# q, k, v and both mLSTM streams split into high and low parts before they go to DRAM

## The chip, the cores and the metric

The kernel runs on one core of a Trainium2 chip. The metric is the device time of one execution in microseconds (us), the median over runs.

## What is computed

One layer of a hybrid encoder for one sequence of 1024 tokens with 1024 channels, in float32: two feed-forward blocks around two sequence mixers. The mixers are a differential attention with 8 heads (two score maps of 64 channels in each, rotary q and k, a block-causal mask over chunks of 64) and an mLSTM with 4 heads of 256 channels.

```
h = x + 1/2 * g1 * SwiGLU_1(mod(rms(x)))
u = mod(rms(h));  P = u @ W_in
...
def mlstm_branch(xm, o_pre, conv_w, conv_b, w_mq, w_mk, w_mv, w_if, b_if, ml_skip, g_mlnorm):
    xc = jax.nn.silu(causal_conv(xm, conv_w, conv_b))
    q = jnp.einsum('bshd,hde->bhse', xch, w_mq)
    k = jnp.einsum('bshd,hde->bhse', xch, w_mk)
    v = jnp.einsum('bshd,hde->bhse', xmh, w_mv)
    ...
    y = (hn + ml_skip.reshape(H, Dh) * xch) * jax.nn.sigmoid(o_pre).reshape(B, S, H, Dh)
...
def diff_attention(q, k, v, lam, g_subln, lambda_init):
    q = rope(q)
    k = rope(k)
    ...
        s = jnp.einsum('bqhcd,bkhcd->bchqk', qi, k) * scale
        p = jax.nn.softmax(s, axis=-1)
        a = p[:, 0] - lam * p[:, 1]
        return jnp.einsum('bhqk,bkhd->bqhd', a.astype(v.dtype), v)
```

## The kernel before

**High and low parts.** A float32 product is done on TensorE as three products of two operands that are each written as a high part (the value rounded to the type fp32r) and a low part (what is left). The three are lines 132, 133 and 134 (`mm3`): high by high, low by high, high by low. A split costs one cast on ScalarE and one subtraction on VectorE. `split` (lines 137 and 138) reads its source from another tile; `split_in` (lines 143 and 144) works on a tile that a load has just filled, and leaves the low part in its place.

**Order.** TensorE's order is the order in which the program is written. ScalarE, VectorE, GpSimd and SyncE's DMA issues are ordered by the tile framework's scheduler. Nearly all DMAs are issued by SyncE (SP), in one order, and one that waits holds up those behind it. A tile that a DMA reads or writes comes free only when that DMA has landed.

**Stages** (times of the profiled execution). The first feed-forward block runs to 693 us. Then `stage_in`: projections to the mLSTM's input xm, channel tile by channel tile. `conv` copies the product from PSUM into `xp`, runs four VectorE passes of a causal convolution into `acc`, a SiLU (line 743) gives xc, and both are split into the four tiles `xh` for the gate products `gates` (lines 754 and 756). The tiles `xh` have one buffer each. xc and xm are stored to DRAM in float32 (lines 746 and 747). The output-gate projections run to 894 us, with the last four `gates` at the half and at the end of the first two of them. The gate chain, a row of small steps and DMAs on the gate values, runs beside these.

From 895 us the mLSTM (`stage_mlstm`) and from 1206 to 1745 us the attention (`stage_attn`) run with dense work (projections to q, k, v and branch gates, in `job_*`) put between their steps: `paced` writes items in the order of due times and dense pieces between them. `mlstm_head` loads 256 tokens of xm or xc at a time, one DMA (line 1051) and one `split_in` for each. `vps` (lines 1084 to 1086) are the products of xm to the mLSTM's values; each is split into `mv`. `job_v` stores the attention's v in float32 (lines 906 and 908), `rotate` the rotated q and k of half the tokens of a head (lines 930 to 945; its inputs `qa` and its three tiles `t`).

In the attention, each head's q goes twice into `Q` (rows 0 to 63 become the high part, 64 to 127 the low part) and k twice into `Kl`, split into `Kh` and `Kl`. The first 256 columns are loaded (line 1245) when the head before has done its last scores with them, the other 768 behind that. Scores `sc` are lines 1276 and 1277; ScalarE's exponential (line 1281) gives `p`; `pt` (line 1305) are transposes of p, which are split into `ah` and `al` (lines 137 and 138) and multiplied with v (`av`) into `po`.

The tiles `t` of 128x512 float32, whoever takes them (`self.t512()`), come from one ring of six buffers.

Of the kernel before, what the change touches and what calls it, by code (L numbers as in the profile page):

```python
# [39 lines left out]
class Halves:  # L40
    """two tiles with half of the tokens each"""
# [9 lines left out]
class Net:  # L51
# [40 lines left out]
    # conditioning: one column block of w_ada per call  # L92
# [27 lines left out]
    # weights  # L120
# [19 lines left out]
    def split_in(self, hi, lo):  # L140
        """the same of what has been loaded into the place of the low part"""
        raw = lo.bitcast(F32)
        self.nc.scalar.copy(hi, raw)
        self.nc.vector.tensor_sub(lo, raw, hi.bitcast(F32))

    def set_lnexp(self, after):
        """have the table set with Ln and Exp loaded behind `after`"""
        t = self.nc.scalar.preload_act_table_set(LNEXP)
        self.after(t, after)
        return t  # L150
# [6 lines left out]
    def rstd_of(self, ps, n, last):  # L157
        """1 / sqrt(ps / n + eps); `last`: the activation before it"""
# [9 lines left out]
    # 1 / rms over channels, on every partition, for some of the tokens  # L168
# [35 lines left out]
    def sum_square(self, n, i, m):  # L204
        """add channel tile m of half n, its i-th, to the running sum of squares"""
        nc = self.nc
        sq = self.t512()
        self.sq_last = nc.scalar.activation(sq, self.h[m][:, n * NW:n * NW + NW], AF.Square)
        if i:
            nc.vector.tensor_add(sq, self.sq_acc, sq)  # L210
        self.sq_acc = sq
# [12 lines left out]
    def norm_step(self, i, q, j, bank):  # L224
        """first half's modulation behind the steps of the last products"""
# [8 lines left out]
    def norm_behind(self, i, n, m, bank):  # L234
        """behind the update of channel tile m of half n: statistics, and the first half's modulation"""
# [12 lines left out]
    def group(self, srcs, psp, tag, hook):  # L248
        """several M-tiles of a projection of u at once, channel tile by channel tile"""
# [15 lines left out]
    def ffn(self, wgu, wd, gt, first, plain, hid, after, step, extra=None):  # L265
        """h += gate * (silu(u w_gate) * (u w_up)) w_down; hidden passes through DRAM"""
# [33 lines left out]
    # The hidden layer goes to DRAM as the operands that down() takes: even tiles are its rows b1., odd ones b2.  # L300
# [9 lines left out]
    def store_right(self, hid, f, c2):  # L310
        """what follows from the second token half of tile f"""
# [8 lines left out]
    def store_left(self, hid, f, c1):  # L320
        """what follows from the first token half, behind store_right"""
# [10 lines left out]
    # One level of Strassen's scheme in Winograd's form: 7 products for the 8 of two tiles of w^T u, with  # L332
    # w^T = [a11 a12; a21 a22] (tiles x channel halves) and u = [b11 b12; b21 b22] (channel x token halves)
# [10 lines left out]
    def combine_u(self, x, pool):  # L344
        """t1 = b12 - b11, t2 = b22 - t1, -t4 = b21 - t2 for one channel tile of each half"""
# [20 lines left out]
    def combine_u3(self, x):  # L366
        """t3 = b22 - b12, in the place of b12"""
# [69 lines left out]
    def down(self, wd, gt, hid, psg, tp, after, step):  # L437
        """the same scheme for w_down^T (channel halves x even and odd tiles) and the hidden layer"""
# [63 lines left out]
        # product: its operands, weights to fetch meanwhile, a combination that takes a weight's place  # L502
# [43 lines left out]
    def first_start(self, srcs, psg, gtag, psd, dtag):  # L546
        """the first block's input: statistics, modulation and the first tiles as x and w_ada come in"""
# [42 lines left out]
    def first_norm(self, i, srcs, psg, gtag, psd, dtag):  # L590
        """later blocks' input: the first tiles run on one half while the other is normalised"""
# [8 lines left out]
    def out_tail(self, n, i, m, bank):  # L600
        """final norm behind the last update of h"""
# [36 lines left out]
    # one M-tile of a projection of u: PSUM halves  # L638
# [18 lines left out]
    def mix_setup(self):  # L657
# [4 lines left out]
                                 for j in range(FT // 2)] for i in range(2))  # L662
# [3 lines left out]
        self.xcd, self.xmd, self.od, self.ybd = ([sc(f"{c}{h}", [P, 2, T]) for h in range(4)]  # L666
                                                 for c in ("xc", "xm", "so", "yb"))
        self.qkd = [sc(f"qk{h}", [2, 2, 2, 32, T]) for h in range(8)]
        self.vd = [sc(f"v{h}", [P, 2, 8, P]) for h in range(4)]
# [4 lines left out]
    def fold_gates(self, hd, psp, tag):  # L674
        """gate weights seen from xc and xm, as [hi | lo] stationary tiles"""
# [32 lines left out]
    def stage_in(self, st):  # L708
        """xm with causal conv and gate pre-activations; sigmoid of the output gate"""
# [15 lines left out]
    def conv_o(self, s1, psd, psg, pre):  # L725
# [3 lines left out]
        def conv(j, ps):  # L729
# [17 lines left out]
            nc.sync.dma_start(out=self.xmd[j // 2][:, j % 2], in_=xp[:, 4:4 + T])  # L747
# [140 lines left out]
    # dense work that fills the tensor engine between the steps of the two sequence mixers  # L888
    def job_v(self, hp):
        nc = self.nc  # L890
        w = [self.unit(self.a["wv"][hp, i]) for i in range(2)]
        for tt in range(8):
# [3 lines left out]
            for k in range(KT):  # L896
# [5 lines left out]
                if k % 2:  # L902
                    if k == KT - 1:
                        if tt % 2 == 0:
                            vo = self.rope.tile([P, 2, 2, P], F32, name=self.nm("vo"), tag=f"vo{tt // 2 % 2}")
                        nc.scalar.copy(vo[:, :, tt % 2], o.rearrange("p (q c) -> p q c", q=2))
                        if tt % 2:
                            nc.sync.dma_start(out=self.vd[hp][:, :, tt - 1:tt + 1], in_=vo)
                    yield 6 * 0.11

    def job_qk(self, hd):
        """rotary q and k of a head"""
# [20 lines left out]
    def rotate(self, hd, ns, a, ps):  # L933
# [10 lines left out]
        for h, t in enumerate((x, a)):  # L944
            nc.sync.dma_start(out=self.qkd[hd][:, :, h].rearrange("q c r t -> (q c) r t")[:, :, ns], in_=t)

    def job_g(self, s, j):
        """pre-activation of a branch gate; for the second one -log of its sigmoid"""
# [29 lines left out]
    def job_b(self, n, m):  # L978
        """gated mLSTM branch of the merge"""
# [19 lines left out]
    def chunk(self):  # L999
        """a piece of the dense work; its time on the tensor engine, 0 when none is left"""  # L1000
# [12 lines left out]
    def paced(self, items):  # L1013
        """emit items (due, time, function) by due time, dense work in between"""
# [29 lines left out]
    def mlstm_head(self, hd, before, pitch, items, m1, m2, psS, psR, psN):  # L1044
# [4 lines left out]
        def load(dst, src, cs):  # L1049
            hi, lo = (x[:, :, cs] for x in dst)  # L1050
            nc.sync.dma_start(out=lo.bitcast(F32), in_=src[:, :, cs])
            self.split_in(hi, lo)

        def load_xc(c):
            load(self.xc, self.xcd[hd], slice(c * 256, c * 256 + 256))

        def begin():
            for c in (3, 2, 1, 0):
                load(self.xm, self.xmd[hd], slice(c * 256, c * 256 + 256))
# [5 lines left out]
        def begin_qk():  # L1065
            """scores of a head: q k^T = xc (w_q w_k^T) xc^T"""
# [114 lines left out]
        # blocks of queries and of keys go from the last to the first, so that the next head's keys and  # L1181
        # values can take the place of those that have had their last use
# [46 lines left out]
    def stage_attn(self, dense):  # L1229
        nc, tc = self.nc, self.tc  # L1230
        nlam, gcol = self.lam[:, 2:3], self.lam[:, 3:4]
        with tc.tile_pool(name="a1", bufs=1) as a1, tc.tile_pool(name="a2", bufs=2) as a2, \
# [7 lines left out]
            def load(hd, part):  # L1240
                """some columns of q (twice, for its high and low parts) and of k (twice)"""
                for x, dst in ((0, qs), (1, kl)):
                    src = self.qkd[hd][x].rearrange("c x r t -> (x r) c t")[:, :, part]
                    for r in (0, 64):
                        nc.sync.dma_start(out=dst[r:r + 64, :, part].bitcast(F32), in_=src)
                self.split_in(kh[:, :, part], kl[:, :, part])
                for o in range(part.start, part.stop, 256):
                    cs = slice(o, o + 256)
                    t = self.t512().rearrange("p (c t) -> p c t", c=2)[64:128]
                    self.split_in(t.bitcast(F32R), qs[64:128, :, cs])  # L1250
                nc.scalar.copy(qs[0:64, :, part], qs[0:64, :, part].bitcast(F32))

            def load_v(hd):
                v = [a2.tile([P, 8, P], F32R, name=self.nm("av"), tag=f"av{i}", bufs=1) for i in range(2)]
                nc.sync.dma_start(out=v[1].bitcast(F32), in_=self.vd[hd // 2][:, hd % 2])
                self.split_in(v[0], v[1])
# [325 lines left out]
```

## Time and profile before

| | |
|---|---|
| time, median of 3 runs | 2677.02 us (2673.28 to 2679.34) |
| span of the profiled execution | 2681.1 us |
| busy: TensorE / VectorE / ScalarE | 97% / 70% / 48% of the span |
| chain that ended last | TensorE 84%, DMA 7%, VectorE 5%, ScalarE 3% |
| granted TensorE clock, mean | 0.990 |

TensorE is busy nearly all the time, so what the kernel can lose or win lies in the places where TensorE stands. The profiled execution is 4.1 us (0.15%) longer than the median of the runs; the page shows no time of it besides its span.

### The profile page before, as it was taken

The page shows a single profiled execution, that of the slowest core. Times are in us where ns is not written, and L with a number is a line of the kernel's source. Part 1 is how long each engine was busy: PE and PEld are TensorE (multiplying, and loading weights), DVE is VectorE, ACT ScalarE, POOL GpSimd, SP SyncE. Part 2 cuts the span into 40 slices and gives each one's busy share as a digit, 9 for nine tenths or more (in the row PEclk, how much of TensorE's full clock was granted, in tenths as well). Part 3 has the DMA queues.
Part 4 walks back from the last instruction along what each step waited for, and adds up shares of the span by engine and source line. Part 5 has one row for each costly group of instructions (what it writes and reads, how often), then busy time and mean ns, then how long its engine had stood idle before and what let it go on. Part 6 is the DMA issues. An engine that isn't in the chain of part 4 may idle for free.

```text
span 2681.1 us, 35203 instructions
## 1 busy us (share of the span) xinstructions
PE 2592.6 (97%) x12704; PEld 2155.8 (80%) x12704; DVE 1877.3 (70%) x3352; ACT 1288.3 (48%) x2369; POOL 22.5 (1%) x85
## 2 busy tenths in 40 slices
PE   6999999999899999999999999999999999999998
PEld 4888887778777799997777778777887888888886
DVE  7987878678795456646766766654467776766867
ACT  6333333446435366654666766753345332323444
POOL 0000000000000000000000000000000000000000
PEclk8999999999999999999999999999999999999999
DMA  7434345833674423334333333558342333236533
GB/s 262 162 130 145 118 149 185 274 99 104 215 258 149 140 91 118 111 100 121 111 102 106 99 105 115 159 198 277 131 140 87 110 98 115 99 102 216 161 95 122
DMA packets 174471, 380.47 MB, mean 142 GB/s; under 512 B 18405, under 2 KB 47529, under 8 KB 174297
## 3 DMA queue, kind: packets, MB, share of 16 engines
q1 hardware_dynamic: 174296, 378.24, 43.6%
q8 instruction: 99, 1.62, 0.2%
q14 instruction: 76, 0.61, 0.1%
HBM read 280.27 MB, written 97.90 MB: 141 GB/s over the span
## 4 chain that ended last, share of the span: by engine, by line
PE 84%; DMA 7%; DVE 5%; ACT 3%; issue 1%; SPq 0%; DVEq 0%; ACTq 0%; POOL 0%; POOLq 0%
PE gu L134 10%; PE gu L133 10%; PE gu L132 10%; PE acc L132 5%; PE acc L133 5%; PE acc L134 5%; PE ab L132 2%; PE ab L133 2%; PE ab L134 2%; PE dn L134 2%; PE dn L132 2%; PE dn L133 2%; PE gp L132 2%; PE gp L134 2%; PE gp L133 2%; PE pt L1305 1%
## 5 line engine op out<-in xcount | busy, mean ns | idle before, releaser
L132 PE MATMUL gu<-uh,wh 128*128 128x512 f32 x800 | 314.2, 393 | 10.1 <-ACT uh L201 8.8
L133 PE MATMUL gu<-ul,wh 128*128 128x512 f32 x800 | 313.4, 392 | 1.3 <-DVE ul L202 1.3
L134 PE MATMUL gu<-uh,wl 128*128 128x512 f32 x800 | 313.2, 391 | 0.8 <-DVE wl L127 0.7
L137 ACT CAST wh<-wr 128x512 fp32r<-128x512 f32 x228 | 134.0, 619 | 253.0 <-PE gu L133 194.0
L132 PE MATMUL acc<-uh,wh 128*128 128x512 f32 x616 | 241.9, 393 | 1.3 <-ACT uh L137 1.3
L133 PE MATMUL acc<-ul,wh 128*128 128x512 f32 x616 | 240.3, 390 | 1.3 <-DVE ul L138 1.3
L134 PE MATMUL acc<-uh,wl 128*128 128x512 f32 x616 | 239.8, 389 | 0.0
L126 ACT CAST wh<-wr 128x1024 fp32r<-128x1024 f32 x120 | 125.8, 1049 | 148.0 <-PE wo L133 46.1
L127 DVE TENSOR_TENSOR wl<-wr,wh 128x1024 fp32r<-128x1024 f32 x120 | 146.5, 1221 | 71.8 <-ACT wh L126 70.9
L132 PEld LDWEIGHTS gu<-uh,wh 128*128 128x128 f32 x800 | 151.2, 189 | 44.3 <-ACT uh L201 10.4
L133 PEld LDWEIGHTS gu<-ul,wh 128*128 128x128 f32 x800 | 151.2, 189 | 34.4 <-DVE ul L202 2.3
L134 PEld LDWEIGHTS gu<-uh,wl 128*128 128x128 f32 x800 | 151.1, 189 | 33.4 <-DVE wl L127 2.3
L133 PE MATMUL gu<-ut,wh 128*128 128x512 f32 x456 | 177.5, 389 | 0.0
L132 PE MATMUL gu<-ut,wh 128*128 128x512 f32 x456 | 177.4, 389 | 0.0
L134 PE MATMUL gu<-ut,wl 128*128 128x512 f32 x456 | 177.4, 389 | 0.0
L138 DVE TENSOR_TENSOR wl<-wr,wh 128x512 fp32r<-128x512 f32 x228 | 152.8, 685 | 1.6 <-ACT wh L137 1.6
L137 ACT CAST uh<-hr 128x512 fp32r<-128x512 f32 x154 | 95.4, 619 | 100.2 <-PE acc L134 63.6
L132 PEld LDWEIGHTS acc<-uh,wh 128*128 128x128 f32 x616 | 115.6, 188 | 28.6 <-ACT uh L137 2.5
L133 PEld LDWEIGHTS acc<-ul,wh 128*128 128x128 f32 x616 | 115.6, 188 | 26.3 <-DVE ul L138 2.2
L134 PEld LDWEIGHTS acc<-uh,wl 128*128 128x128 f32 x616 | 115.6, 188 | 24.1
L138 DVE TENSOR_TENSOR ul<-hr,uh 128x512 fp32r<-128x512 f32 x154 | 105.8, 687 | 35.5 <-ACT uh L137 35.0
L1281 ACT ACTIVATE p<-sc,lr 128x256 f32<-128x256 f32 (+7 forms) x128 | 94.8, 741 | 74.0 <-DVE lr L1279 72.1
(335 smaller groups left out, 6561.4 us busy)
## 6 DMA issues: line engine op xcount, KB each, us to landing
ada<-wada SPq DMA_DIRECT2D x72, 512.0 KB
wr<-win SPq DMA_DIRECT2D x48, 512.0 KB
wr<-w1gu SPq DMA_DIRECT2D x44, 512.0 KB
wr<-w2gu SPq DMA_DIRECT2D x44, 512.0 KB
wr<-wab SPq DMA_DIRECT2D x32, 512.0 KB
g<-t SPq DMA_DIRECT2D x32, 256.0 KB
t<-g SPq DMA_DIRECT2D x32, 256.0 KB
wr<-wout SPq DMA_DIRECT2D x16, 512.0 KB
```

What stands on the lines that cost most here:

```text
L126: nc.scalar.copy(hi, raw)
L127: nc.vector.tensor_sub(lo, raw, hi.bitcast(F32))
L132: nc.tensor.matmul(ps, w[0], x[0], start=start, stop=False)
L133: nc.tensor.matmul(ps, w[0], x[1], start=False, stop=False)
L134: nc.tensor.matmul(ps, w[1], x[0], start=False, stop=stop)
L137: (eng or self.nc.scalar).copy(hi, src)
L138: self.nc.vector.tensor_sub(lo, src, hi.bitcast(F32))
L1281: nc.scalar.activation(pc[c][:, 0:W], ps[:, 0:W], AF.Exp, bias=lr[:, 2 + c:3 + c], accum_out=lr[:, c:c + 1])
L1305: nc.tensor.transpose(pt[:, kk, i], a[i][:, kb * P:kb * P + P], self.ident)
```

## The change

xc and xm are stored as high and low parts by `conv`, from the tiles `xh` that the gate products read (xc also as before, since a later step reads it whole). q and k are split in `rotate`, v in `job_v`, and both parts are stored. The loads fetch high and low parts into their places and split nothing. The diff, without its lines that only take out comments:

```diff
-        self.xcd, self.xmd, self.od, self.ybd = ([sc(f"{c}{h}", [P, 2, T]) for h in range(4)]
-                                                 for c in ("xc", "xm", "so", "yb"))
-        self.qkd = [sc(f"qk{h}", [2, 2, 2, 32, T]) for h in range(8)]
-        self.vd = [sc(f"v{h}", [P, 2, 8, P]) for h in range(4)]
+        self.xcd, self.od, self.ybd = ([sc(f"{c}{h}", [P, 2, T]) for h in range(4)] for c in ("xc", "so", "yb"))
+        self.xcs, self.xms = ([[sc(f"{c}{p}{h}", [P, 2, T]) for p in "hl"] for h in range(4)] for c in ("xc", "xm"))
+        self.qkd = [[sc(f"qk{p}{h}", [2, 2, 2, 32, T]) for p in "hl"] for h in range(8)]
+        self.vd = [[sc(f"v{p}{h}", [P, 2, 8, P]) for p in "hl"] for h in range(4)]
...
             nc.sync.dma_start(out=self.xcd[j // 2][:, j % 2], in_=acc)
-            nc.sync.dma_start(out=self.xmd[j // 2][:, j % 2], in_=xp[:, 4:4 + T])
+            for p in range(2):
+                nc.sync.dma_start(out=self.xcs[j // 2][p][:, j % 2], in_=xh[p].bitcast(F32))
+                nc.sync.dma_start(out=self.xms[j // 2][p][:, j % 2], in_=xh[2 + p].bitcast(F32))
             return xh
...
                         if tt % 2 == 0:
-                            vo = self.rope.tile([P, 2, 2, P], F32, name=self.nm("vo"), tag=f"vo{tt // 2 % 2}")
-                        nc.scalar.copy(vo[:, :, tt % 2], o.rearrange("p (q c) -> p q c", q=2))
+                            vo = [self.t512().rearrange("p (q t c) -> p q t c", q=2, t=2) for _ in range(2)]
+                        self.split(o.rearrange("p (q c) -> p q c", q=2),
+                                   *(x.bitcast(F32R)[:, :, tt % 2] for x in vo))
                         if tt % 2:
-                            nc.sync.dma_start(out=self.vd[hp][:, :, tt - 1:tt + 1], in_=vo)
+                            for x, d in zip(vo, self.vd[hp]):
+                                nc.sync.dma_start(out=d[:, :, tt - 1:tt + 1], in_=x)
...
-        for h, t in enumerate((x, a)):
-            nc.sync.dma_start(out=self.qkd[hd][:, :, h].rearrange("q c r t -> (q c) r t")[:, :, ns], in_=t)
+        for h, (t, hi) in enumerate(((x, y), (a, b))):
+            self.split(t, hi.bitcast(F32R), t.bitcast(F32R))
+            for p, o in enumerate((hi, t)):
+                nc.sync.dma_start(out=self.qkd[hd][p][:, :, h].rearrange("q c r t -> (q c) r t")[:, :, ns], in_=o)
...
         def load(dst, src, cs):
-            hi, lo = (x[:, :, cs] for x in dst)
-            nc.sync.dma_start(out=lo.bitcast(F32), in_=src[:, :, cs])
-            self.split_in(hi, lo)
+            for x, d in zip(dst, src):
+                nc.sync.dma_start(out=x[:, :, cs].bitcast(F32), in_=d[:, :, cs])
...
-                for x, dst in ((0, qs), (1, kl)):
-                    src = self.qkd[hd][x].rearrange("c x r t -> (x r) c t")[:, :, part]
-                    for r in (0, 64):
-                        nc.sync.dma_start(out=dst[r:r + 64, :, part].bitcast(F32), in_=src)
-                self.split_in(kh[:, :, part], kl[:, :, part])
-                for o in range(part.start, part.stop, 256):
-                    cs = slice(o, o + 256)
-                    t = self.t512().rearrange("p (c t) -> p c t", c=2)[64:128]
-                    self.split_in(t.bitcast(F32R), qs[64:128, :, cs])
-                nc.scalar.copy(qs[0:64, :, part], qs[0:64, :, part].bitcast(F32))
+                src = [[d[x].rearrange("c x r t -> (x r) c t")[:, :, part] for d in self.qkd[hd]] for x in range(2)]
+                for r in range(2):
+                    rows = slice(64 * r, 64 * r + 64)
+                    for dst, o in ((qs, src[0][r]), (kh, src[1][0]), (kl, src[1][1])):
+                        nc.sync.dma_start(out=dst[rows, :, part].bitcast(F32), in_=o)
...
-                nc.sync.dma_start(out=v[1].bitcast(F32), in_=self.vd[hd // 2][:, hd % 2])
-                self.split_in(v[0], v[1])
+                for x, d in zip(v, self.vd[hd // 2]):
+                    nc.sync.dma_start(out=x.bitcast(F32), in_=d[:, hd % 2])
```

Counted over the whole program, ScalarE has 71 instructions fewer after the change, VectorE 24 fewer, SyncE issues 144 DMAs more; TensorE's and GpSimd's rows are the same in the same order. Three places show how the other engines' orders move.

ScalarE where the mLSTM begins, before (`wv` are the weights of the first `vps`, `qa` a copy for `rotate`, `wh` a dense weight's high part):

```order
L137 CAST wv_7581<-wr_7579 128x512
L1037 CAST mv_7563<-onz 128x8x2
L1037 CAST mv_7564<-zeros 128x8x2
L927 COPY qa_7628<-qp_7603 128x512
L143 CAST xm_7559<-xm_7560 128x2x256
L143 CAST xc_7561<-xc_7562 128x2x256 x4
L143 CAST xm_7559<-xm_7560 128x2x256 x2
L927 COPY qa_7655<-qp_7630 128x512
L143 CAST xm_7559<-xm_7560 128x2x256
L126 CAST wh_7916<-wr_7914 128x1024
L137 CAST mv_7563<-vps_7676 128x256
```

ScalarE at the same place after the change:

```order
L137 CAST wv_7625<-wr_7623 128x512
L1044 CAST mv_7611<-onz 128x8x2
L1044 CAST mv_7612<-zeros 128x8x2
L932 COPY qa_7668<-qp_7643 128x512
L932 COPY qa_7695<-qp_7670 128x512
L137 CAST mv_7611<-vps_7716 128x256
L137 CAST mv_7611<-vps_7725 128x256
L137 CAST mv_7611<-vps_7734 128x256
L137 CAST mv_7611<-vps_7743 128x256
```

The eight casts of `xm` and `xc` are gone from the front of the first `mv`, and the weight cast `wh` that stood right in front of the first `mv` has moved behind the eight `mv`.

SyncE in `stage_in` before, around the fifth and sixth channel tile (`ada` are columns of the conditioning weights, `wr` a projection's weights):

```order
L746 DMA xc2_303<-acc_1170_6492 128x1024
L114 DMA ada_1261_7367<-wada 128x1024
L124 DMA wr_1235_7148<-win 128x1024
L114 DMA ada_1262_7372<-wada 128x1024
L747 DMA xm2_307<-xp_1176_6568 128x1024
L114 DMA ada_1263_7377<-wada 128x1024
L114 DMA ada_1270_7442<-wada 128x1024
L746 DMA xc2_303<-acc_1181_6576 128x1024
L114 DMA ada_1271_7447<-wada 128x1024
```

SyncE at the same place after the change:

```order
L124 DMA wr_1235_7196<-win 128x1024
L114 DMA ada_1252_7340<-wada 128x1024
L114 DMA ada_1253_7345<-wada 128x1024
L747 DMA xc2_303<-acc_1181_6615 128x1024
L749 DMA xch2_317<-xh_1166_6522 128x1024
L750 DMA xmh2_325<-xh_1168_6524 128x1024
L749 DMA xcl2_318<-xh_1167_6523 128x1024
L750 DMA xml2_326<-xh_1169_6525 128x1024
L749 DMA xch2_317<-xh_1177_6609 128x1024
L750 DMA xmh2_325<-xh_1179_6611 128x1024
L749 DMA xcl2_318<-xh_1178_6610 128x1024
L750 DMA xml2_326<-xh_1180_6612 128x1024
```

Where the stores of two channel tiles stood between loads, the high and low parts of the fifth (`xh_1166` to `xh_1169`) and of the sixth (`xh_1177` to `xh_1180`) now follow one another, and the loads of `ada` and of the next weights have moved behind them.

SyncE at the start of the attention's second head, before:

```order
L1245 DMA Kl_11949<-qk_318 64x2x256 x2
L1245 DMA Q_11947<-qk_318 64x2x768 x2
L1245 DMA Kl_11949<-qk_318 64x2x768 x2
L945 DMA qk_320<-t_12620 4x32x512
L124 DMA wr_13236<-win 128x1024
L945 DMA qk_320<-qa_12464 4x32x512
L1245 DMA Q_11947<-qk_319 64x2x256 x2
```

SyncE at the same place after the change:

```order
L1252 DMA Kh_12040<-qkh_333 64x2x256
L1252 DMA Kl_12041<-qkl_334 64x2x256
L1252 DMA Kh_12040<-qkh_333 64x2x256
L1252 DMA Kl_12041<-qkl_334 64x2x256
L1252 DMA Q_12039<-qkh_333 64x2x768
L1252 DMA Kh_12040<-qkh_333 64x2x768
L1252 DMA Kl_12041<-qkl_334 64x2x768
L1252 DMA Q_12039<-qkl_334 64x2x768
L1252 DMA Kh_12040<-qkh_333 64x2x768
L1252 DMA Kl_12041<-qkl_334 64x2x768
L1252 DMA Q_12039<-qkh_335 64x2x256
L1252 DMA Q_12039<-qkl_336 64x2x256
```

The first 256 columns of k take four issues where they took two, the other 768 columns of q and k take six where they took four, and the next head's first columns of q follow directly.

## Rows read from the trace of the kernel before

**Rows 1.** The page's head and its busy times (engine, busy us, share, instructions).

```profile
span 2681.1 us, 35203 instructions
...
PE 2592.6 (97%) x12704; PEld 2155.8 (80%) x12704; DVE 1877.3 (70%) x3352; ACT 1288.3 (48%) x2369; POOL 22.5 (1%) x85
```

**Rows 2.** Who waited for whom, TensorE: us in total, times, longest us.

```profile
PE pt L1305 <- DVE al L138: 9.2, 9, 2.2
...
PE vps L1084 <- DVE mv L138: 3.3, 3, 1.8
PE sc L1277 <- DVE Kl L144: 3.1, 7, 0.7
...
PE po L133 <- DVE al L138: 2.2, 3, 1.8
PE sc L1276 <- ACT Kh L143: 2.0, 4, 1.1
...
PE oss L1345 <- ACT t L162: 1.8, 1, 1.8
```

**Rows 3.** Timeline where the attention's second head needs its other columns of q.

```profile
1303.36 1.90 DVE L144 TENSOR_TENSOR Q<-Q,t 64x512 fp32r<-64x512 f32 x3 [0.15 <-ACT t L143]
...
1304.10 0.44 PE L1276 MATMUL sc<-Kh,Q 128*128 128x384 f32 x1 [2.49 <-DVE Q L144]
```

**Rows 4.** Timeline behind the start of the sixth head.

```profile
1565.08 1.48 ACT L143 CAST Kh<-Kl 128x1536 fp32r<-128x1536 f32 x1
...
1566.34 0.90 PE L1305 MATMUL pt<-ident,p 128*128 128x128 f32 x3 [2.24 <-DVE al L138]
```

**Rows 5.** Windows: busy us (instructions) of each engine, granted clock, DMA share, GB/s.

```profile
1453.60:1460.40 6.80, 5.47 (x15) 4.54 (x16) 5.39 (x11) 3.31 (x8) 0.00 (x0) 0.50 0.44 94
1566.30:1569.80 3.50, 3.46 (x12) 3.04 (x13) 3.14 (x6) 1.15 (x3) 0.00 (x0) 0.52 0.46 150
```

**Rows 6.** Timeline at the second head's start.

```profile
1279.63 1.28 SPq L1245 DMA_DIRECT2D Kl<-qk  x2
...
1283.55 0.62 ACT L143 CAST Kh<-Kl 128x512 fp32r<-128x512 f32 x1
```

**Rows 7.** Groups by line and form in the attention: count, busy us, mean ns.

```profile
L144 DVE TENSOR_TENSOR Q<-Q,t 64x512 fp32r<-64x512 f32 x31 | 21.1, 687 | 7.4 <-ACT t L143 6.8
...
L938 DVE TENSOR_TENSOR t<-qa,cos 128x512 f32<-128x512 f32 x14 | 9.6, 682 | 0.0
```

**Rows 8.** Timeline of ScalarE in the attention.

```profile
1378.87 0.69 ACT L162 ACTIVATE t<-oss,epsc 128x512 f32<-128x512 f32 x1 [3.60 <-DMA qk<-t]
```

**Rows 9.** Windows by stage.

```profile
759.00:829.00 70.00, 70.00 (x308) 51.16 (x306) 66.29 (x106) 36.49 (x43) 0.51 (x5) 1.00 0.69 241
...
1205.00:1222.00 17.00, 15.76 (x70) 12.40 (x69) 7.24 (x9) 8.81 (x13) 0.34 (x2) 1.00 0.85 242
1222.00:1745.00 523.00, 497.91 (x2530) 411.36 (x2528) 367.40 (x705) 349.31 (x643) 6.15 (x30) 0.99 0.38 111
```

**Rows 10.** Timeline where the mLSTM begins.

```profile
911.10 1.22 DVE L127 TENSOR_TENSOR wl<-wr,wh 128x1024 fp32r<-128x1024 f32 x1 [0.26 <-ACT wh L126]
...
912.71 0.39 PE L1084 MATMUL vps<-wv,xm 128*128 128x256 f32 x1 [1.76 <-DVE mv L138]
...
917.67 0.38 PE L1084 MATMUL vps<-wv,xm 128*128 128x256 f32 x1 [1.36 <-DVE mv L138]
```

**Rows 11.** Timeline in `stage_in`, from one group of gate products to the next.

```profile
804.74 0.40 PE L754 MATMUL gps<-xh,G 128*16 128x512 f32 x1
...
809.46 1.22 DVE L138 TENSOR_TENSOR xh<-xp,xh 128x1024 fp32r<-128x1024 f32 x1
...
812.07 0.40 PE L754 MATMUL gps<-xh,G 128*16 128x512 f32 x1
```

**Rows 12.** DMA in the stretch from 735 to 831 us.

```profile
DMA packets 6484, 23.65 MB, mean 246 GB/s; under 512 B 720, under 2 KB 720, under 8 KB 6480
...
q1 hardware_dynamic: 6480, 23.60, 70.5%
```

More of the change, by code (lines that the diff above doesn't have):

```diff
@@ L1049, in load @@
         def load(dst, src, cs):
-            hi, lo = (x[:, :, cs] for x in dst)
-            nc.sync.dma_start(out=lo.bitcast(F32), in_=src[:, :, cs])
-            self.split_in(hi, lo)
+            for x, d in zip(dst, src):
+                nc.sync.dma_start(out=x[:, :, cs].bitcast(F32), in_=d[:, :, cs])
         def load_xc(c):
-            load(self.xc, self.xcd[hd], slice(c * 256, c * 256 + 256))
+            load(self.xc, self.xcs[hd], slice(c * 256, c * 256 + 256))
         def begin():
             for c in (3, 2, 1, 0):
-                load(self.xm, self.xmd[hd], slice(c * 256, c * 256 + 256))
+                load(self.xm, self.xms[hd], slice(c * 256, c * 256 + 256))
             raw = self.wraw.tile([P, D], F32, name=self.nm("wr"), tag="raw")[:, 0:512]
```

## The prediction

> **What bounds the kernel now.** I read the page first, then the list of TensorE's waits, then the timeline around each long one, and the windows by stage last. The page shows TensorE busy for 2592.6 of 2681.1 us [rows 1], and the change leaves TensorE's rows and their order as they are. So it can only take away places where TensorE stands, or add some. In the attention TensorE is busy for 497.91 of 523 us: it stands for 25.1 us [rows 9]. The list of waits says for whom [rows 2]. The waits for Kl and Kh are splits of a load, and so is the one wait for Q, of 2.49 us [rows 3]. The waits for `al` are not: `al` is the low part of the transposed scores, made in any case. The timeline shows why it is late. In the sixth head ScalarE had casts of a load to do, the last of them 1.48 us for the other columns of Kh, the high part `ah` had to queue among them, and the transposes behind `al` started 2.24 us late [rows 4]. So the splits of loads cost mostly by delaying other work on the two engines that do them.
>
> **Attention, what goes.** ScalarE loses a cast for each load, a copy and four casts for each head's Q; VectorE loses 31 subtractions of 0.687 us for Q in this stage alone [rows 7], and those for K and v. What TensorE gets back of that:
>
> The wait for Q goes, since nothing is left between the landing and the scores: -2.5 us [rows 3].
>
> The waits for `al` are 9.2 + 2.2 = 11.4 us in twelve places [rows 2]. The one of 2.24 us is behind a load's cast and goes [rows 4]. The one of 1.8 us comes behind a split of v, six passes of `rotate` and the normalisation of a head at once; I count half. Of the other 7.4 us I count a third, since `rotate` and the row sums crowd the same engines. That is 2.2 + 0.9 + 2.5 = 5.6, taken as -5.5 us; the ends are 0 (other work moves into the gap) and -8.
>
> Behind each of these two long waits TensorE's granted clock fell to its lower level, 1.2 of 2.4 GHz: 0.50 for 6.8 us and 0.52 for 3.5 us [rows 5]. At half speed half of such a stretch is lost, 3.4 and 1.7 us. The second goes with its wait, the first I leave: -1.7 us, ends 0 and -5.1.
>
> The waits for Kh and Kl at the heads' starts, 2.0 + 3.1 = 5.1 us [rows 2], I leave whole. Before, two issues take 1.28 us, both have landed 3.92 us after the first issue began (1283.55 less 1279.63), and the cast takes 0.62 us [rows 6]: Kh is there at 4.54, Kl with a subtraction of about 0.69 [rows 7] at 5.2. After, four issues at 0.64 us go out as Kh, Kl, Kh, Kl. A load that lands as long after its own issue as the second did, 3.28 us, brings the second Kh at 1.28 + 3.28 = 4.56 and the second Kl at 5.2. The issues cost what the split cost: 0, ends -5.1 and the rival below.
>
> **Attention, what comes.** 14 of the 16 halves of `rotate` run here [rows 7], each with two subtractions and two casts more. 28 subtractions of 0.68 us are 19 us of VectorE, less than the 21.1 us that Q alone gives back, so the engine is not busier. But a burst of six passes becomes one of eight, 1.4 us longer, and whatever queues behind it is later by that. If it hits TensorE's path once it costs 1.4 us: I take +1.5, ends 0 and +6 (four times).
>
> The three tiles `t` of each half are now all held until a store has landed, where one was. ScalarE has waited 3.60 us for such a store before [rows 8], and TensorE 1.8 us behind it [rows 2]. SyncE's queue is longer at a head's start, and such a store stands behind it. I take +0.5, ends 0 and +4. Loads of v go from one to two, with no split; weight loads, which now stand behind more of SyncE's issues, are issued well ahead of their use: 0.
>
> Sum for the attention: -2.5 - 5.5 - 1.7 + 0 + 1.5 + 0.5 = -7.7 us.
>
> **Start of the mLSTM.** The three waits of `vps` for `mv` are 3.3 us [rows 2]. VectorE does a weight's low part, 1.22 us, right before `mv` is due, and `vps` waits 1.76 us; a second wait of 1.36 us follows among the splits of the last xm blocks [rows 10]. After the change the weight's cast stands behind the `mv` and the splits are gone. The first xm low part is only the ninth load that SyncE issues, so one wait may be replaced by another: -2.5 us, ends -3.3 and +1.3 (two issues at 0.64 us). Inside the mLSTM no wait for a split of xc or xm is long enough to matter: 0. The 32 subtractions for v lie beside TensorE's work there: 0.
>
> **From mLSTM to attention.** The DMA engines are busy for 0.85 of these 17 us [rows 9], and now the last v, in two parts, and the first Q, Kh, Kl, v meet there, with the tiles `t` held until v's stores have gone out. +1 us, ends 0 and +3.
>
> **`stage_in`.** Here the change adds: three stores of 0.52 MB more for each of eight channel tiles, 12.6 MB beside the 23.65 MB of this stretch [rows 12]. The tiles `xh` have one buffer, so the next tile's split waits until these stores have landed. While TensorE does a whole projection between two groups of gate products there is room. The last four groups are 7.33 us apart (812.07 less 804.74), and the split before ends at 810.68, 1.39 us ahead [rows 11]. Five stores are 2.62 MB. The DMA engines moved 246 GB/s at a busy share of 0.705, so 349 GB/s while they work [rows 12]: 7.5 us for five stores. That is just about the step, the high parts land first and can be overwritten first, and the order has moved `ada` and a weight load out from between. So +1 us, ends 0 and +12 (the rival below). The gate chain's DMAs come later by the queue, but the output-gate projections run beside it.
>
> **Sum.** -7.7 - 2.5 + 1 + 1 = -8.2 us. Against the profiled 2681.1 that is 2672.9; the median of the runs lies 4.1 us lower: 2668.8, taken as **2669 us**. Differences within 0.2%, 5.4 us, are about what a measurement of this kernel can't tell from no change.
>
> **Rivals.**
> *Other work takes the gap.* The bursts of `rotate` and the ring of `t` keep `al` as late as it is but for the one wait of 2.2: -2.5 - 2.2 - 1.7 + 2.8 + 1.8 in the attention, -2.5 + 2 elsewhere, together -2.3: about 2675 us, no change. For it speaks that VectorE's busy share there stays at two thirds; against it that the long waits have a load's split right before them.
>
> *The stores hold `stage_in`.* At the mean 246 GB/s instead of 349, five stores take 10.7 us, and the last subtraction of 1.22 us follows the last landing: 11.9 us for a step of 7.33. Three steps lose 13.7, less 1.4 of slack: +12 instead of +1, about 2680 us. It starts to cost when the last of a tile's stores lands later than 1.2 us before its gate products. VectorE is busy for 66.29 of 70 us there [rows 9], which leaves little to catch up with.
>
> *Twice the loads land one behind another.* If the four loads at a head's start take as long each as the first two on average (3.92 / 2 = 1.96 us), the fourth lands at 7.8 us instead of 5.2: +2.6 us at each of seven starts, 18 us, about 2687 us, slower. It decides from the point where the fourth lands later than 5.2 us after the first issue. Against it: the second load landed within 3.28 us of its issue, so the two overlapped, and the DMA engines are busy for 0.38 of the attention [rows 9]. The Trainium skill, "DMA: Bandwidth & Descriptors", speaks for it and against the change: section "Anatomy of one DMA — SWDGE (gpsimd) path" gives a DMA that GpSimd issues a fixed price of about 2.0 us besides its bytes, and "Rules for kernel authors" asks to put many small transfers together. As an estimate by that page, the 144 DMAs more, one behind another, would cost 288 us; the trace bears it out in part: the second load took 3.28 us from its issue, but it was issued 0.64 us behind the first [rows 6].
>
> *More comes back.* The `al` waits give 8, both clock drops 5.1, `mv` 3.3, and K 2: 8.5 us more, about 2660 us.
>
> **How the numbers follow.** The forecast 0.42, its own range 2663 to 2675; other work in the gap 0.24; `stage_in` 0.14; loads one behind another 0.07; more comes back 0.13. Faster by over 0.2% (below 2671.7): three quarters of the first and all of the last, 0.45. Slower (above 2682.4): the loads, a third of `stage_in`, and 0.06 for costs at both bounds, 0.18. The rest, 0.37, is no change. For 8 in 10 the range leaves out the loads, the worst of `stage_in` and the best of the last: 2657 to 2684 us.
>
> **What would show it.** Right: in the attention no wait for Q, half of the waits for `al` gone, TensorE standing for about 17 us instead of 25.1; no `vps` wait over 0.5 us; the last gate groups 7.3 us apart. Wrong: `gps` waits of some us for `xh` (stores), `sc` waits of over 1 us for DMA at the heads' starts (loads), or ScalarE waiting for stores of q and k more often than before (the ring).

## The result, and the profile after

The change made the kernel slower: 2692.02 us (2689.51 to 2695.41) against 2678.18 us of the kernel before in the same session, a ratio of 1.0057 with an interval of 1.0045 to 1.0069. The profiled execution took 2693.7 us, 12.6 more than before. Its head and busy times, from the page:

```profile
span 2693.7 us, 35395 instructions
...
PE 2599.2 (96%) x12704; PEld 2162.6 (80%) x12704; DVE 1840.1 (68%) x3328; ACT 1236.0 (46%) x2298; POOL 22.5 (1%) x85
```

VectorE and ScalarE did become less busy, as the counts say, and TensorE still stands for longer. TensorE's instructions come in the same order in both kernels, so the same instruction can be looked up in both and its two times compared. The timeline of the changed kernel, at the instructions shown before in [rows 11] (`gps`), [rows 10] (`vps`), [rows 3] (`sc`) and [rows 4] (`pt`):

```profile
801.72 0.40 PE L757 MATMUL gps<-xh,G 128*16 128x512 f32 x1
...
809.05 0.40 PE L757 MATMUL gps<-xh,G 128*16 128x512 f32 x1
...
907.86 0.38 PE L1090 MATMUL vps<-wv,xm 128*128 128x256 f32 x1 [0.21 <-DVE mv L138]
...
912.01 0.39 PE L1090 MATMUL vps<-wv,xm 128*128 128x256 f32 x1 [0.21 <-DVE mv L138]
...
1318.61 0.42 PE L1277 MATMUL sc<-Kh,Q 128*128 128x384 f32 x1
...
1582.15 0.66 PE L1306 MATMUL pt<-ident,p 128*128 128x128 f32 x4
```

The two gate groups start 3.0 us earlier than before (801.72 for 804.74), still 7.33 us apart. The last `vps` shown is 5.7 us earlier (912.01 for 917.67). The scores of the second head are 14.5 us later (1318.61 for 1304.10), the transposes of the sixth head 15.8 us (1582.15 for 1566.34). So some 20 us go lost between the start of the mLSTM and the second head. The windows narrow it down; each begins and ends at the same instruction of TensorE in both kernels. First the changed kernel (busy time of TensorE, its weight loads, VectorE, ScalarE and GpSimd, then granted clock, DMA share, GB/s), then the kernel before:

```profile
1222.24:1332.60 110.36, 88.22 (x416) 72.00 (x414) 67.17 (x140) 49.62 (x101) 0.82 (x4) 0.92 0.49 145
1332.60:1758.02 425.42, 415.02 (x2114) 343.48 (x2114) 270.90 (x540) 265.15 (x507) 5.36 (x26) 0.99 0.52 151
```

```profile
1222.16:1311.81 89.65, 82.47 (x416) 68.10 (x414) 69.42 (x139) 51.68 (x102) 0.82 (x4) 1.00 0.35 98
1311.81:1746.24 434.43, 415.28 (x2115) 343.14 (x2113) 299.00 (x568) 298.88 (x545) 5.33 (x26) 0.99 0.39 114
```

At the attention's start the lead of 5.7 us is gone: the instruction of 1222.16 comes at 1222.24. In the first stretch TensorE stands for 22.1 us (110.36 less 88.22) where it stood for 7.2, and its granted clock falls to a mean of 0.92, so that the same 416 instructions also keep it busy 5.8 us longer (88.22 for 82.47). The stretch takes 20.7 us more than before. In the rest of the stage TensorE stands for 10.4 us where it stood for 19.2, and the rest takes 9.0 us less. The gain that was forecast is there, behind a loss that is larger. Who TensorE waits for, in the whole changed kernel:

```profile
PE oss L1346 <- ACT t L162: 6.6, 2, 6.1
PE sc L1277 <- ACT p L1282: 6.6, 2, 3.7
PE pt L1306 <- DVE al L138: 6.1, 5, 2.8
...
PE pt L1306 <- DVE p L1289: 4.2, 1, 4.2
...
PE qp L132 <- DVE t L138: 2.5, 1, 2.5
PE num L1141 <- ACT sch L137: 2.5, 1, 2.5
PE po L133 <- DVE al L138: 1.5, 2, 1.2
...
PE sc L1278 <- DMA Kl<-qkl: 1.0, 5, 0.3
...
PE vps L1090 <- DVE mv L138: 0.6, 3, 0.2
```

Against [rows 2], the waits for a split of Q, Kh or Kl are gone (1.0 us is left for Kl's own loads), and those of `vps` are 0.6 for 3.3. New are waits for ScalarE: for `p`, and for the tile `t` of a head's normalisation. What ScalarE itself waited for in the attention, of the changed kernel, from its list of waits:

```profile
ACT qa L932 <- DMA qkl<-qa: 16.5, 4, 6.0
...
ACT wh L126 <- DMA wr<-win: 9.8, 2, 7.2
...
ACT t L162 <- DMA qkh<-t: 6.3, 2, 4.7
...
ACT t L162 <- DMA qkl<-t: 5.2, 1, 5.2
...
ACT t L970 <- DMA qkh<-t: 2.0, 1, 2.0
ACT t L1339 <- DMA qkl<-t: 1.9, 2, 1.5
...
ACT t L1339 <- DMA qkh<-t: 0.2, 1, 0.2
```

Six rows of stores of q and k, 32.1 us in all. The same list of the kernel before has the 3.6 us of [rows 8] and two rows more, 10.0 us in all:

```profile
ACT qa L927 <- DMA qk<-qa: 5.7, 2, 3.3
...
ACT t L143 <- DMA qk<-t: 0.7, 1, 0.7
```

It is eleven waits where there were four. Half of the 32.1 us is for `qa`, which has a buffer of its own for each half and is not of the ring. One such wait in the timeline of the changed kernel:

```profile
1245.62 0.59 ACT L932 COPY qa<-qp 128x512 f32<-128x512 f32 x1 [3.20 <-DMA qkl<-qa]
1246.10 0.51 ACT L1288 ACTIVATE p<-p,lr 128x256 f32<-128x256 f32 x1
...
1246.64 0.48 DVE L1289 SCALAR_TENSOR_TENSOR p<-p,lr,p 128x256 f32<-128x256 f32 x1 [3.82 <-ACT p L1288]
...
1247.18 0.90 PE L1306 MATMUL pt<-ident,p 128*128 128x128 f32 x3 [4.18 <-DVE p L1289]
```

ScalarE's next instruction is the copy into `qa`, a tile whose last content is still on its way to DRAM. It stands for 3.2 us, the scaling of `p` queues behind it, VectorE waits for that, and TensorE stands for 4.18 us.

Not all of it is a held tile. The first long wait of TensorE in this stretch, 3.70 us, comes from the 9.8 us of waits for weight loads in the list above, where the kernel before has 1.5 us. ScalarE stood for 7.21 us until a load of weights had landed, and the exponential queued behind it:

```profile
1240.40 1.04 ACT L126 CAST wh<-wr 128x1024 fp32r<-128x1024 f32 x1 [7.21 <-DMA wr<-win]
...
1241.96 0.51 PE L1277 MATMUL sc<-Kh,Q 128*128 128x384 f32 x1 [3.70 <-ACT p L1282]
```

The last load of these weights before it went out at 1231.10, between stores of q and k that went out from 1229.74 to 1232.90. So it landed about 9 us after its issue, if not later; in e1 below, such loads land after a median of 4.1 us. That the stores held it up is argued from this difference.

Why are the stores so slow? Windows in which hardly any but q and k stores are under way, of the changed kernel and of the kernel before:

```profile
1278.50:1284.50 6.00, 6.00 (x34) 5.22 (x33) 6.00 (x12) 3.07 (x6) 0.00 (x0) 1.00 0.26 102
```

```profile
1243.00:1246.00 3.00, 3.00 (x15) 2.48 (x14) 1.88 (x6) 1.50 (x5) 0.00 (x0) 1.00 0.26 81
```

The mean busy share of the 16 DMA engines is 0.26, about 4 of 16, for as long as this lasts. At 102 GB/s a store of 256 KB takes 2.6 us, and the four of one half of `rotate` 10.3 us where two took 5.1. The store's outermost dimension in DRAM is 4 (`(q c) r t`, 4 x 32 x 512).

### The profile page after: what moved, and what is told of

It is laid out like the page before. It is cut to its first block, busy times and chain, and to the rows that moved or that the text cites. A ratio compares the mean times of both kernels' runs of the same rounds, so it can differ in the third digit from the quotient of the medians.

```text
span 2693.7 us, 35395 instructions
## 1 busy us (share of the span) xinstructions
PE 2599.2 (96%) x12704; PEld 2162.6 (80%) x12704; DVE 1840.1 (68%) x3328; ACT 1236.0 (46%) x2298; POOL 22.5 (1%) x85
## 4 chain that ended last, share of the span: by engine, by line
PE 85%; DMA 7%; DVE 4%; ACT 3%; issue 1%; SPq 1%; DVEq 0%; ACTq 0%
PE gu L134 10%; PE gu L133 10%; PE gu L132 10%; PE acc L132 5%; PE acc L133 5%; PE acc L134 5%; PE ab L132 2%; PE ab L133 2%; PE ab L134 2%; PE gp L132 2%; PE gp L133 2%; PE gp L134 2%; PE dn L134 2%; PE dn L133 2%; PE dn L132 2%; DMA qkl<-qa 1%
## 5 line engine op out<-in xcount | busy, mean ns | idle before, releaser
L132 PEld LDWEIGHTS gu<-uh,wh 128*128 128x128 f32 x800 | 151.5, 189 | 44.4 <-ACT uh L201 10.4
```

Source lines behind the costliest of these rows:

```text
L132: nc.tensor.matmul(ps, w[0], x[0], start=start, stop=False)
```

## Experiments

The kernels and their medians, in us, and their ratios to the kernel before in the same session:

| q, k split | streams, v split | narrow stores (outermost 4) | wide stores (128 rows) |
|---|---|---|---|
| no | no | before: 2678, 1 | e2: 2662, 0.9936 |
| no | yes | e3: 2671, 0.9976 | e11: 2661, 0.9926 |
| yes | no | e4: 2689, 1.0038 | e8: 2650, 0.9902 |
| yes | yes | the change: 2692, 1.0057 | e1: 2650, 0.9889 |
| no, stores issued twice | no | e9: 2703, 1.0093 | e10: 2660, 0.9937 |

Theory N (narrow stores) says that this width, doubled in bytes, is the loss. Theory R says that it is the ring of tiles and SyncE's longer queue, whatever the transfers take. The layouts below change only the order of rows; the loads of q and k take 64 rows that follow one another in all of them.

**e1: the changed kernel with wide stores.** The two rotary halves change places with the 32 rows, so that a store's 128 rows are one dimension. q and k get the same other order of rows, which leaves their products as they are.

```diff
-        self.qkd = [[sc(f"qk{p}{h}", [2, 2, 2, 32, T]) for p in "hl"] for h in range(8)]
+        self.qkd = [[sc(f"qk{p}{h}", [2, 2, 32, 2, T]) for p in "hl"] for h in range(8)]
-   out=self.qkd[hd][p][:, :, h].rearrange("q c r t -> (q c) r t")[:, :, ns]
+   out=self.qkd[hd][p][:, :, :, h].rearrange("q c r t -> (q c r) t")[:, ns]
-   d[x].rearrange("c x r t -> (x r) c t")
+   d[x].rearrange("c r x t -> (r x) c t")
```

> The changed kernel with another layout of the q and k scratch in DRAM: the two rotary halves stand inside each channel pair, so that a store is 128 rows in one dimension and no longer 4 x 32 rows; loads take the rows in the same other order for q and k, so the scores are the same sums. Theory N (narrow stores): stores of 2048-byte packets alone move 102 GB/s at a DMA share of 0.26, a quarter of the 16 engines, so four of 256 KB take over 10 us, and ScalarE, whose next tile waits for them, holds up p and ah. Then this kernel gets back most of the 20 us lost where the attention starts: 2671 to 2677 us, and ScalarE's waits for q and k stores fall from 16.5 and 4.7 us there to under 5 in all. Theory R (the ring of six tiles and SyncE's longer queue, whatever the transfers take): 2688 to 2693 us.

Measured: 2649.63 us, ratio 0.9889 (0.9875 to 0.9903). That is 42 us below the change, at least twice what theory N expected, and theory R is refuted. A window of its stores, and the attention:

```profile
936.00:937.50 1.50, 1.50 (x15) 1.50 (x14) 0.61 (x2) 0.73 (x2) 0.00 (x0) 1.00 0.93 344
1222.00:1745.00 523.00, 514.29 (x2661) 428.14 (x2660) 356.27 (x704) 330.01 (x628) 6.18 (x30) 1.00 0.52 157
```

The stores now run at a share of 0.93 and 344 GB/s. TensorE stands for 8.7 of 523 us, and its clock stays at 1.00. ScalarE's waits for q and k stores in this stage are 2.2 us, those for weight loads 2.8.

```profile
ACT t L162 <- DMA qkl<-t: 1.4, 1, 1.4
...
ACT qa L932 <- DMA qkl<-qa: 0.8, 1, 0.8
```

**e2: the kernel before with wide stores**, the same edit on its one scratch for each head.

> The kernel before with the same layout of the q and k scratch and nothing else. Theory N: its two stores a half are as narrow, ScalarE waited 5.7 us for qa at the attention's start and 3.6 us for a tile later, so 2 to 7 us are gained: 2671 to 2676 us. Theory R: no change, 2676 to 2680 us.

Measured: 2662.19 us, ratio 0.9936 (0.9923 to 0.9949), 16.6 us less. More than expected: the kernel before paid for narrow stores too, in waits that I had put down to other things. None of ScalarE's 10.0 us for stores is left in the attention, and TensorE's waits for `al` fall from 11.4 us to 7.4. With wide stores on both sides the change is a gain: e1 is 12.6 us below e2.

**e3: the changed kernel with q and k as before** (the two functions of the diff that store and load them taken back), and **e4: the kernel before with only q and k changed.**

> The changed kernel with q and k stored in float32 and split at their loads as before; the mLSTM's streams and v stay split at their source. If q and k carry the loss: 2672 to 2678 us, with the gain of 3 to 5 us by the mLSTM's start kept and none of the 22 us lost from 1222 to 1330 us. If the streams' or v's stores carry it: 2688 us or more.

> The kernel before with only q and k stored as high and low parts. If q and k carry the loss, 2690 to 2698 us. If the streams or v carry it, 2670 to 2678 us.

Measured: e3 2671.41 us, ratio 0.9976 (0.9964 to 0.9987). e4 2689.33 us, ratio 1.0038 (1.0025 to 1.0052), just below what was expected. The loss is q's and k's. The streams and v by themselves gain some. The two ratios together would make 1.0014 and not the change's 1.0057, so the parts also act on each other; how was not found.

**e5: the changed kernel with stores of 8 x 16 rows.** Three dimensions for the 32 rows and the halves, in an order that makes the store's outermost dimension 8.

```diff
+        self.qkd = [[sc(f"qk{p}{h}", [2, 2, 2, 2, 16, T]) for p in "hl"] for h in range(8)]
+   out=self.qkd[hd][p][:, :, :, h].rearrange("q c s r t -> (q c s) r t")[:, :, ns]
+   d[x].rearrange("c s x r t -> (s x r) c t")
```

> The changed kernel with a q and k scratch whose stores are 8 x 16 rows (4 x 32 in the change, 128 rows in one dimension in e1); loads again take rows of q and k in the same order. Theory N says that the size of the outermost dimension sets how many of the 16 DMA engines a store uses: with 8, stores alone move about 200 GB/s at a share of about 0.5, and the time lies between the change and e1, nearer to e1: 2655 to 2672 us. If it is not the width but something else of e1's layout (rows that follow one another in DRAM), it stays at 2685 us or more, or falls to e1's 2650 whatever the 8.

Measured: 2660.91 us, ratio 0.9941 (0.9926 to 0.9956). A window of its stores:

```profile
936.50:938.50 2.00, 2.00 (x19) 2.00 (x18) 0.85 (x2) 0.54 (x2) 0.00 (x0) 1.00 0.52 200
```

Outermost dimension 4, 8 and 128 give shares of 0.26, 0.52 and 0.93, and 2692, 2661 and 2650 us. The time follows the width.

**e6: the change's own layout, each store in four DMAs of 32 rows.**

```diff
+                for i in range(4):
+                    nc.sync.dma_start(out=self.qkd[hd][p][i // 2, i % 2, h][:, ns], in_=o[32 * i:32 * i + 32])
```

> The changed kernel with its own layout in DRAM, but each store of q and k in four DMAs of 32 rows, 192 DMAs more. Theory N: 32 rows go to all 16 engines, so the time comes near e1's in spite of four times the stores, less what SyncE's issues of some 0.5 us each cost: 2650 to 2665 us. Theory L (the layout, not the width): 2685 us or more. Theory C (each DMA has a price that adds up): above 2692 us.

Measured: 2683.29 us, ratio 1.0023 (1.0013 to 1.0034), 9 us below the change, far above what theory N expected and in none of the three ranges. ScalarE's waits for stores are nearly gone, but not the time. Its list of waits in the attention, then TensorE's longest wait there, then SyncE's issues of these stores (count: shortest, median, longest ns):

```profile
ACT wh L126 <- DMA wr<-win: 11.0, 3, 7.5
...
ACT t L971 <- DMA qkl<-qa: 0.3, 1, 0.3
```

```profile
PE gp L132 <- ACT wh L126: 10.5, 1, 10.5
```

```profile
L953 SPq DMA_DIRECT2D qkh<-t x128: 302/422/1773, 923.0 to 1611.3; - x128
```

Each small store is quick, and its issue takes 0.42 us all the same. Sixteen for a half are 6.7 us of SyncE, a load of weights behind them is late, and TensorE stands for 10.5 us at once. Theories N and C are both right in a part: quick transfers free the tiles, and the number of issues has its own price in the queue. How much of the 34 us over e1 is that price was not separated.

**e7: e1 with v as before**, and **e8: e2 with only q and k split at their source.**

> e1 with v stored in float32 and split at its load as before; q, k and the streams stay split at their source. If splitting v at its source is worth something with wide stores: 2652 to 2657 us. If it costs (TensorE waits 2 us for v's split at 1199 us in e1, and its tiles hold the ring): 2644 to 2648 us.

> The kernel before with only q and k split at their source and with e1's layout. If q and k bring most of the 12.5 us between e2 and e1: 2651 to 2656 us. If the streams and v bring most: 2658 to 2663 us.

Measured: e7 2647.44 us, ratio 0.9885 (0.9869 to 0.9900); e8 2650.15 us, ratio 0.9902 (0.9887 to 0.9918). e1, e7 and e8 can't be told apart. With wide stores q and k alone bring all of the gain. e7 is the lowest median, 31 us below the kernel before.

**e9: the kernel before with each q and k store issued twice**, the second into a scratch that is not read, and **e10: the same with wide stores.** No split or load is touched, so this is the suspected cost by itself.

```diff
-            nc.sync.dma_start(out=self.qkd[hd][:, :, h].rearrange("q c r t -> (q c) r t")[:, :, ns], in_=t)
+            for d in (self.qkd, self.qkx):
+                nc.sync.dma_start(out=d[hd][:, :, h].rearrange("q c r t -> (q c) r t")[:, :, ns], in_=t)
```

> The kernel before with each store of q and k issued twice, the second into a scratch that nothing reads; no split moves, loads stay as they were. It doubles the suspected cost alone. Theory N: four narrow stores a half, as in the change: 10 to 25 us more than before, most of it at the attention's start, with ScalarE waiting over 10 us for q and k stores. If instead the splits added in rotate or the other loads made the loss: within 4 us of before, 2674 to 2682 us.

> The same doubling with e2's layout, so that all four stores a half are wide. Theory N: the same bytes and the same number of stores cost next to nothing on 16 engines, 2661 to 2668 us, against 2662 of e2. If it is the number of stores or the bytes and not their width: 10 us or more above e2, 2672 us or more.

Measured: e9 2703.04 us, ratio 1.0093 (1.0079 to 1.0107), 25 us more than before. e10 2660.44 us, ratio 0.9937 (0.9923 to 0.9951), the same as e2. Twice the bytes in twice the stores cost 25 us on a quarter of the DMA engines and nothing on all of them. ScalarE's waits in the attention of e9:

```profile
ACT qa L927 <- DMA qx<-qa: 18.3, 4, 5.7
...
ACT Q L1252 <- DMA Q<-qk: 11.2, 7, 6.8
...
ACT t L162 <- DMA qx<-t: 5.9, 1, 5.9
...
ACT t L143 <- DMA qx<-t: 2.6, 1, 2.6
```

The waits for loads of Q grow too: 11.2 us, where the kernel before and e10 both have 6.0. So narrow stores delay loads as well as hold tiles. How the loss divides between the two is open; no run gives the tiles more buffers.

**e11: e2 with the streams and v split at their source, q and k not.**

> e2 with the mLSTM's streams and v split at their source (q and k stay in float32, their stores wide): the last corner of the four combinations. If the parts add up, e11 less e2 is what e3 showed against before, about -7 us, so 2654 to 2657 us; if the streams and v bring only what q and k bring as well when both are there (e1 and e8 differ by 0.5 us), it lies between, and e1 less e11 is less than the 12 us that q and k bring alone.

Measured: 2661.28 us, ratio 0.9926 (0.9911 to 0.9941), not to be told from e2's 0.9936. The parts do not add up: what the streams and v brought in e3, beside narrow stores, they do not bring beside wide ones. One price is in the traces: at the end of the mLSTM TensorE waits for the split of v at its source (`qp` for `t`) for 2.8 us in e11, 2.1 in e1, 2.5 in e3 and in the change, and not at all in e2, e7 and e8, which store v in float32. e3 pays it as well, so it does not explain the difference, which stays open.

## Why the prediction was wrong

**The step that failed** is the term for the ring in the attention: "I take +0.5, ends 0 and +4". It said that the tiles of `rotate` are held until a store has landed and that one store more per tile would cost little. The mechanism was named and the rows for it were there [rows 8], but its size was wrong: the same doubling alone costs 25 us over the whole kernel (e9). In the changed kernel ScalarE waits 32.1 us for stores of q and k in the attention, 22.1 more than before. The term counted the tiles `t` alone; half of those waits are for `qa`, which one store held before as after, only that this store now comes behind three others. And the term for weight loads, put at 0 since they are issued well ahead of their use, was wrong: 9.8 us of ScalarE's waits, one of them with 3.70 us of TensorE's behind it. ScalarE waiting for stores more often than before was the sign that the prediction gave for the ring.

I took the 3.60 us wait as one event and never asked how long a store of 256 KB ought to take. The mean rate of `stage_in`, 349 GB/s, would give 0.75 us; the stores of q and k have 2.6. The trace of before showed it, in the window of 0.26 above. With it the sum would have had a store burst of 10.3 us in each of 14 halves, against a copy to `qa` that waits for the last of them. What a burst costs TensorE can't be read from that alone. The rival of the ring and the bursts had the right place and a price of a few us; the rival of twice the loads looked at the loads of q and k, for which TensorE waits 1.0 us in all (Kl). The parts of the rival in which more comes back add up to 8.7 us and not 8.5, which leaves its 2660 us.

**Q**, -2.5 us: right, no wait for it is left.

**`al`**, -5.5 us of 11.4: 7.6 us are left in the changed kernel, some of them behind ScalarE's waits for stores, and in e1 4.3, which is 7.1 us less. The list of e1:

```profile
PE pt L1306 <- DVE al L138: 3.6, 4, 1.9
...
PE po L133 <- DVE al L138: 0.7, 1, 0.7
```

**Kh and Kl**, 0 of 5.1 us: too careful. 1.0 us is left in the changed kernel and 1.3 in e1, so some 4 us came back. In e1 the loads of 128 KB land after a median of 2.8 and 3.0 us, not after the 3.28 us that I carried over.

**The clock**, -1.7 us: the other way. The mean fell to 0.92 in the stretch where TensorE stood most, which kept TensorE busy 5.8 us longer there, and stayed at 0.99 in the rest. The lower level came with the waits: around those of 3.70 and 4.18 us the clock was 0.50 from 1242.2 to 1252.4 us. In e1, where TensorE waits for 1.9 us at most in the attention, the mean is 1.00.

**`rotate`'s bursts**, +1.5 us: nothing of this size is seen. e8, which has them, stands lower than e2, which has not; since e8 also loses the splits at the loads, no run takes the bursts by themselves.

**Start of the mLSTM**, -2.5 us: right, and at its size. The waits of `vps` for `mv` fall from 3.3 us to 0.6, and between [rows 11] and [rows 10] the changed kernel gains 2.6 us (5.66 less 3.02).

**Inside the mLSTM**, 0: wrong. The whole lead of 5.7 us is lost between [rows 10] and the attention's start. TensorE waits once for 2.5 us (`num`, in the list above) behind ScalarE, which waits for tiles held by stores of q, k and v:

```profile
954.91 0.42 ACT L1158 ACTIVATE t<-t 128x256 f32<-128x256 f32 x1 [2.08 <-DMA qkh<-t]
958.17 0.47 ACT L1157 ACTIVATE t<-num,den 128x256 f32<-128x256 f32 x1 [2.74 <-DMA vh<-t]
```

It is the same mechanism: two of the halves of `rotate` run here. In e1 TensorE has no such wait for `num`.

**From mLSTM to attention**, +1 us for crowded DMA engines: it is 2.5 us, and for another reason. TensorE waits for v's split at its source (`qp` for `t`, in the list above), and still does for 2.1 us in e1; the 32 subtractions for v had been put at 0.

**`stage_in`**, +1 us with a rival at +12: no cost. The last gate groups are 7.33 us apart as before, with 29.84 MB at 311 GB/s and a share of 0.832 in the same stretch as [rows 12]. That is 6.2 MB more, where the prediction had added 12.6, since loads of `ada` have left the stretch:

```profile
DMA packets 8189, 29.84 MB, mean 311 GB/s; under 512 B 915, under 2 KB 915, under 8 KB 8185
...
q1 hardware_dynamic: 8185, 29.78, 83.2%
```

Most of the 3.0 us by which the gates are early came from before them: TensorE's longest wait for a weight of these projections was 3.8 us where it had been 5.4, and the first block was 0.8 us shorter; neither is the change's doing as far as the trace tells.

**Twice the loads, one behind another** did not happen. A price for each DMA did not add up where the stores were wide: e10 issues 32 stores more than e2 (four for each of 16 halves where two stood) and takes the same time. The Trainium skill, "DMA: Bandwidth & Descriptors", section "Anatomy of one DMA — SWDGE (gpsimd) path", gives about 2.0 us as the fixed price of a DMA that GpSimd issues. These are issued by SyncE, and nothing like 2.0 us for each shows in e10's time.

## What to carry to other kernels

Before more bytes go through an existing store or load, look up its rate in the trace: a stretch in which it runs almost alone, and what share of the DMA engines that stretch has. A share that sits at a quarter while stores follow one another can be a transfer that runs on a quarter of them, as here, and another order of dimensions in a scratch that only the kernel sees can mend it. A wait for a tile is priced by how long the transfer behind it takes when it is doubled, not by the wait's length today; ask too which loads will run beside it. Moving a split off the load paid here only when the stores that it added were cheap.

## What the hardware showed that I had not expected

A store with an outermost dimension of 4 moved 102 GB/s at a share of 0.26, with 8 it was 200 GB/s at 0.52, with 128 rows 344 GB/s at 0.93, for tiles of the same bytes and partitions. The Trainium skill has this rule on the very page that I had cited: "DMA: Bandwidth & Descriptors", section "Why a DMA increments its semaphore by 16 and not by 1", says that a DMA uses the largest number of engines up to 16 that divides the slowest dimension of both sides. The three shares, 0.26, 0.52 and 0.93 of 16, agree with 4, 8 and 16 engines.

The issue of such a store on SyncE also depended on its form: 0.55 us for 4 x 32 rows, 0.58 for 8 x 16, 0.32 for 128 rows in one dimension (medians; the first line of each kernel's list for this store, the change, e5 and e1).

```profile
L952 SPq DMA_DIRECT2D qkh<-t x32: 508/550/4497, 926.8 to 1622.5; - x32
```

```profile
L952 SPq DMA_DIRECT2D qkh<-t x32: 570/583/1297, 923.9 to 1587.5; - x32
```

```profile
L952 SPq DMA_DIRECT2D qkh<-t x32: 319/320/955, 924.9 to 1578.9; - x32
```
